# A hybrid S5 and attention layer on one core: written order kept on TensorE alone during the projection, and casts near the attention's end fixed behind their loads

## The chip, the core and the metric

The kernel runs on one core of a Trainium2 chip. The core has five engines with a queue of their own each: TensorE (PE, matrix multiplications, with its weight loads shown as PEld), VectorE (DVE), ScalarE (ACT), GpSimd (POOL) and SyncE (SP), which here only issues transfers between the chip's memory and the core. An engine works through its queue in order: an instruction that waits for another engine or for a transfer holds everything behind it. The metric is the time of one execution in microseconds of device time.

## The reference

One step of a layer with two branches. A normalised and modulated input of 2048 + 64 rows is projected to 3080 columns: the S5 input u, two gates, q, k, v and 8 forget logits. The S5 branch (32 groups with a diagonal complex state) goes through a scan, a GELU and a gated linear unit (GLU); the attention branch has 8 heads with normalised q and k and a cumulative forget bias. Both are gated, joined, projected again and added to the input.

```python
h = _rmsnorm(x, norm_g) * (1.0 + scale[:, None, :]) + shift[:, None, :]
proj = h @ w_in
u, z_s, q, k, v, z_a, f_logit = jnp.split(proj, IN_SPLITS, axis=-1)
...
y_ssm = jax.nn.gelu(y_ssm)
y_ssm = y_ssm * jax.nn.sigmoid(y_ssm @ w_glu.astype(f32) + b_glu.astype(f32))
y_ssm = (y_ssm * jax.nn.silu(z_s.astype(f32))).astype(x.dtype)
q = _rmsnorm(q.reshape(n_b, n_t, N_HEADS, HEAD_DIM), q_norm_g)
k = _rmsnorm(k.reshape(n_b, n_t, N_HEADS, HEAD_DIM), k_norm_g)
...
cum = jnp.cumsum(logf, axis=1)
...
mixed = jnp.concatenate([y_ssm, y_att], axis=-1)
y = x + gate[:, None, :] * (mixed @ w_out)
```

## The kernel before, in words

The program text is traced in order, and then a scheduler puts each engine's instructions into a queue, by a list in which an instruction is taken when the scheduler's model holds it ready. Three means fix an order against it. `ordered()` (L331) chains the instructions of its block on every engine to one another, so that each queue is the written order. `Chain.strict` (L137) does this for TensorE alone. `keep_in_program_order` fixes a single instruction behind the one that was written before it on its engine.

The stages in the order of time:

- Up to about 130 us: loading and normalising the input, and the first u columns.
- About 130 to 808 us: `InProj.line` (L627) works through 22 stretches of the projection, each a set of 256 columns of u, k, v, q or z for half of the rows. A set of weights is loaded by `fetch` (L516) into two buffers `wst`, and cut into a high and a low part by `part` (L529), four pairs of tiles: ACT casts `whi` (L310), DVE subtracts to `wlo` (L312). A block of 128 rows takes 24 matmuls, three for each of 8 slices, and its result goes to one of three banks `low2` to `low4`. `natural` (L585) evicts k and q blocks: ACT squares (L618), DVE and POOL make the power `qss` (L317, L318), DVE multiplies (L622, L623), SP writes. It evicts v blocks by a copy (L612). `channels` (L558) evicts u (L570) and z (L580, then a write to `z_d`, L581).
- Between the blocks, `line` takes steps of `rest()`, the side work: the S5 setup and 16 sets, the end of the scan, the forget logits (with the round trip of `lf` through memory), the attention's bias, and eight steps `operands` (L1615). Each of these loads four quarter blocks `b` of the output weights (L1623), adds and subtracts them, casts them to `ph` and `pl`, and writes eight tiles `t` back to memory (L1636).
- The whole of that stands in `with e.ordered()` in the kernel before.
- From 808 us: the GLU (weights `wgs`, cast to `wgh` and `wgl`) and the attention, with TensorE strict. Here `weights` (L1644) takes steps between the attention's units: it loads blocks `ost` in a ring of three buffers, casts them on ACT to `ohb` (L310), subtracts on POOL to `olb` (L196), then does the same with `m0`, split into `mha11` and `mha21`, and with the decode rows (`decode_load`, L1815). The attention's exponentials `p` run on ACT (L343).
- From about 1311 us: the output projection, in written order on all engines.

Of the kernel before, what the change touches and what calls it, by code (L numbers as in the profile page):

```python
# [21 lines left out]
DEC = 64  # L22
# [158 lines left out]
def Step(tc, a, o, ctx):  # L181
# [3 lines left out]
    V, S, PL, PE = nc.vector, nc.scalar, nc.gpsimd, Chain(tc, nc.tensor, nosync)  # L185
# [116 lines left out]
    V.memset(lf, 0.0)  # L302
    cm = cst.tile([P, H, 21], F32, name="cm")

    def split(x, hi, lo, eh=None, el=None):
        eh = eh or S
        if eh is V:
            V.tensor_copy(hi, x)
        else:
            S.copy(hi, x)  # L310
        if el is V:
            V.tensor_tensor(lo, x, hi, op=ALU.subtract)  # L312
        else:
            padd(lo, x, hi, ALU.subtract)
# [817 lines left out]
class Attn:  # L1132
# [332 lines left out]
    def run(self, out):  # L1465
# [59 lines left out]
        while not out.near:  # L1525
            next(weights)
# [67 lines left out]
class Out:  # L1594
# [12 lines left out]
    def __init__(self, e):  # L1607
        self.e = e
        self.mem = Region(e.nc)
        self.pre = Region(e.nc, R_PRE)  # L1610
        self.b, self.a, self.x, self.acc, self.tmp, self.gate = {}, {}, {}, {}, {}, {}
        self.d = []
        self.near = False

    def operands(self, k, n):  # L1615


        e = self.e
        pre = self.pre
        ns = slice(256 * n, 256 * n + 256)  # L1620
        b11, b12, b21, b22 = (pre.tile([P, 256], F32, name="b%d%d" % (i, j), bufs=1) for i in range(2) for j in range(2))
        for i, b in enumerate((b11, b12, b21, b22)):
            e.nc.sync.dma_start(b, self.block(i // 2, i % 2, k)[:, ns])  # L1623
        yield
        yield
        t2 = pre.tile([P, 256], F32, name="t2", bufs=1)
        e.V.tensor_tensor(b22, b22, b12, op=ALU.subtract)
        e.padd(b12, b12, b11, ALU.subtract)
        e.V.tensor_tensor(t2, b22, b11, op=ALU.add)
        e.padd(b21, b21, t2, ALU.subtract)  # L1630
        yield
        for t, x in (("t3", b22), ("t1", b12), ("t2", t2), ("t4", b21)):
            hl = [pre.tile([P, 256], F32R, name="p" + i, bufs=4) for i in "hl"]
            e.split(x, *hl, el=e.V)
            for i in range(2):
                e.nc.sync.dma_start(e.t_d[t][k, i][:, ns], hl[i].bitcast(F32))  # L1636
# [7 lines left out]
    def weights(self):  # L1644


        e = self.e
        mem = self.mem
        blocks = [(i, j) for i in range(2) for j in range(2)]

        def wait(n):
            while mem.room(2048) < n:
                yield

        yield from wait(5)
        mem.ring("ost", 2048, 3)
        late = []

        def part():
            st, key = late.pop(0)  # L1660
            h, l = (mem.tile([P, 512], F32R, name="o%s%s%d" % ((x,) + key)) for x in "hl")
            e.split(st, h, l)
            self.b[key] = h, l

        for k in range(4):
            for i, j in blocks:
                yield from wait(2)
                if len(late) == 2:
                    part()
                st = mem.tile([P, 512], F32, name="ost")  # L1670
                e.nc.sync.dma_start(st, self.block(i, j, k))
                late.append((st, ("b%d%d" % (i + 1, j + 1), k)))
                yield
        while late:
            yield from wait(2)
            part()
            yield
        for x in "hl":
            for name, n in (("a11", 1), ("a12", 1), ("a22", 2), ("s4", 1)):
                yield from wait(n)  # L1680
                mem.ring("m" + x + name, 2048, n)
            mem.rings["m%sa21" % x] = mem.rings["m%ss4" % x]
        while mem.room(4096) < 2:
            yield
        for j in range(2):
            mem.ring("m%d" % j, 4096, 1)
        self.load(0, 0)
        yield
        for name in ("a11", "a21"):
            self.split(0, name)  # L1690
            yield
        for j in range(2):
            yield from wait(2)
            mem.ring("ms%d" % (j + 1), 2048, 1)
            mem.ring("m%ss1" % "hl"[j], 2048, 1)
            self.decode_load(j)
            yield
        for s in (1, 0):
            for n in (1, 0):
                if s == n == 0:  # L1700
                    yield from wait(1)
                g = self.gate[s, n] = mem.tile([P, 512], F32, tag="ost" if s or n else "gate", name="gate", bufs=1)
                e.nc.sync.dma_start(g, e.gt_d[s, 512 * n:512 * n + 512].partition_broadcast(P))
        for i in (16, 0, 1):
            while mem.room(4096) < 1:
                yield
            mem.ring("x", 4096, 1)
            self.residual(i)
            yield
        self.load(1, 0)  # L1710
        self.near = True
        for t, n in (("t2", 4), ("t1", 4), ("t3", 3)):
            for k in range(n):
                yield from wait(2)
                self.fetch(t, k)
                yield
# [42 lines left out]
        if n == 4:  # L1759
            e.V.tensor_tensor(s, a12, self.a[p, "s2"], op=ALU.subtract)  # L1760

    def split(self, p, *names):
        for name in names:
            hi, lo = (self.mem.tile([P, 4, P], F32R, tag="m" + x + name, name="m" + x) for x in "hl")
            self.e.split(self.a[p, name], hi, lo, el=self.e.V)
            self.a[p, name] = hi, lo

    def multiply(self, acc, a, b, first=True):
# [46 lines left out]
    def decode_load(self, j):  # L1815

        e = self.e
        m = self.mem.tile([P, 4, DEC], F32, tag="ms%d" % (j + 1), name="md%d" % j)
        for k in range(4):
            e.nc.sync.dma_start(m[:, k].rearrange("p (t c) -> p t c", t=TC), (e.ms_d, e.ma_d)[j][P * k:P * k + P, :, NCH:])  # L1820
        hl = self.mem.tile([P, 4, P], F32R, tag="m%ss1" % "hl"[j], name="mhl")
        e.S.copy(hl[:, :, :DEC], m)
        e.V.tensor_tensor(hl[:, :, DEC:], m, hl[:, :, :DEC], op=ALU.subtract)
        self.d.append(hl)

# [89 lines left out]
def body(tc, a, o):  # L1915
    with ExitStack() as top:
        e = Step(tc, a, o, top)
# [3 lines left out]
        ip = InProj(e)  # L1921
# [40 lines left out]
                yield from out.operands(*divmod(i, 2))  # L1962

        side = rest()
        with e.ordered():
            ts = [("u", 0, 0, (2, 3), 3, None), ("u", 256, 256, (2, 3), 3, None)]
            for half in ((2, 3), (0, 1)):
                for i, (kind, base, row) in enumerate(ip.PARTS):
                    after = (lambda g: ip.get(g - 2)) if half[0] and i == 9 else None
                    ts.append((kind, base, row, half, {"v": 2, "z": 1.5}.get(kind, 1), after))  # L1970
            ip.line(ts, side)
            left = sum(1 for _ in side)
            assert left < 12, left
            print('LEFT', left)
        at = made[0]
        low.close()
        e.psum = fixed
        e.PE.strict = True
        with ExitStack() as es:
            at.twins = e.banks(es, "twin", 2, 1024)  # L1980
            with ExitStack() as es2:
# [35 lines left out]
```

## Time and profile before

| | us |
|---|---|
| median of three runs (lowest, highest) | 1513.54 (1513.40, 1518.99) |
| the profiled execution | 1513.53 |
| its span | 1511.8 |
| around the span | 1.7 |

A row of a timeline or a chain gives the start and the length in microseconds, the engine, the line, the operation with its result and its operands, and in brackets how long the engine had been idle and what ended that. A row of the waits gives the total, how often, and the longest. "PEq" and "SPq" are the sequencers of these engines. A granted clock of 1.00 is TensorE's full speed.

### The profile page before, as it was taken

The numbers are of one execution on the slowest core, as the hardware profiler recorded it, in microseconds if no ns is written. First come the engines' busy times: TensorE is split into PE (matmuls) and PEld (weight loads), VectorE is DVE, ScalarE is ACT, GpSimd is POOL, SyncE is SP. The second block draws the span as 40 slices with busy tenths as digits, with TensorE's granted clock in tenths as the row PEclk, the third lists the DMA queues.
The fourth block names the chain that finished last, engine by engine and source line by source line (L and its number), as shares of the span: only waits on it lengthen the run. The fifth ranks groups of instructions, "written<-read, shape, count | busy, mean of one in ns | idle before, by whom it ended". The sixth has DMA issues, their size and how long they took to land.

```text
span 1511.8 us, 25816 instructions
## 1 busy us (share of the span) xinstructions
PE 1351.2 (89%) x9160; PEld 1055.0 (70%) x9160; DVE 967.3 (64%) x2404; ACT 600.3 (40%) x1641; POOL 474.5 (31%) x444
## 2 busy tenths in 40 slices
PE   5887978989999889998975989999999989798998
PEld 2885977989889788996854865555555444376887
DVE  2637857767766468654342788787687676355775
ACT  3645223444433344443322435545544435431221
POOL 1101045235312143332113312433413426324443
PEclk9899989999999899999977989999999999898999
DMA  9756312332345623433569862324122222367452
GB/s 342 298 181 183 94 43 85 122 94 86 92 122 163 232 83 96 124 105 110 174 217 287 252 169 66 92 59 134 47 64 57 57 65 72 94 205 245 158 164 87
DMA packets 249472, 204.90 MB, mean 136 GB/s; under 512 B 91295, under 2 KB 217339, under 8 KB 248320
## 3 DMA queue, kind: packets, MB, share of 16 engines
q1 hardware_dynamic: 249344, 203.27, 43.4%
q8 instruction: 72, 1.18, 0.3%
q14 instruction: 56, 0.46, 0.1%
HBM read 137.68 MB, written 65.53 MB: 134 GB/s over the span
## 4 chain that ended last, share of the span: by engine, by line
PE 46%; DMA 6%; DVE 5%; issue 2%; ACT 2%; POOL 1%; SPq 1%; ACTq 0%; DVEq 0%; POOLq 0%
PE twin L145 12%; PE bank L145 11%; PE low L145 9%; PE last L145 8%; PE glu L145 2%; DVE pb L1359 2%; PE bank L148 2%; DMA ost<-in_w_out_dram 1%; DMA wst<-in_w_in_dram 1%; DMA ms_d<-gx 1%; DMA b<-in_w_out_dram 1%; POOL olb L196 1%; DMA m<-ma_d 1%; ACT p L343 1%; DVE acc L1436 0%
## 5 line engine op out<-in xcount | busy, mean ns | idle before, releaser
L145 PE MATMUL low<-whi,h 128*128 128x256 f32 (+1 forms) x1584 | 303.7, 290 | 13.7 <-DVE ev L622 8.2
L145 PE MATMUL low<-h,whi 128*128 128x256 f32 (+2 forms) x1152 | 279.6, 335 | 17.8 <-ACT whi L310 6.2
L145 PEld LDWEIGHTS low<-whi,h 128*128 128x128 f32 x1584 | 254.6, 194 | 17.0 <-issue 9.6
L145 PE MATMUL low<-wlo,h 128*128 128x256 f32 (+1 forms) x816 | 233.1, 288 | 9.0 <-DVE wlo L312 9.0
L1359 DVE CUSTOM_DVE_ANT_0 pb<-twin,cb 128x512 bf16<-128x512 f32 (+3 forms) x328 | 200.0, 610 | 63.3 <-PE twin L145 53.9
L145 PEld LDWEIGHTS low<-h,whi 128*128 128x128 f32 x1152 | 199.4, 195 | 38.1 <-ACT whi L310 6.9
L343 ACT ACTIVATE p<-twin 128x1024 f32<-128x1024 f32 (+3 forms) x180 | 149.6, 839 | 117.6 <-PE twin L145 106.9
L145 PE MATMUL low<-h,wlo 128*128 128x256 f32 (+2 forms) x576 | 190.1, 331 | 1.0 <-DVE wlo L312 1.0
L145 PEld LDWEIGHTS low<-wlo,h 128*128 128x128 f32 x816 | 158.3, 194 | 11.2 <-DVE wlo L312 10.8
L145 PE MATMUL bank<-p,vt 128*64 128x512 f32 (+3 forms) x704 | 146.0, 538 | 0.0
L318 POOL TENSOR_TENSOR qss<-qss,mhalf 128x4 f32<-128x4 f32 (+1 forms) x68 | 76.5, 1125 | 208.7 <-DVE qss L317 207.3
L145 PE MATMUL twin<-qs,ks 64*128 64x512 f32 (+3 forms) x1056 | 134.6, 360 | 0.0
L145 PEld LDWEIGHTS low<-h,wlo 128*128 128x128 f32 x576 | 112.3, 195 | 11.0 <-DVE wlo L312 2.2
L1436 DVE TENSOR_TENSOR acc<-acc,p 128x1024 f32<-128x1024 f32 (+4 forms) x90 | 89.5, 995 | 37.5 <-ACT p L343 35.6
L312 DVE TENSOR_TENSOR wlo<-wst,whi 128x512 fp32r<-128x512 f32 (+1 forms) x96 | 70.9, 766 | 50.9 <-ACT whi L310 50.7
L145 PEld LDWEIGHTS twin<-qs,ks 64*128 64x128 f32 x1056 | 95.4, 192 | 11.2
L145 PE MATMUL twin<-sm,kb 64*128 64x512 f32 (+3 forms) x360 | 78.5, 431 | 26.5 <-DVE pm L1359 13.8
L618 ACT ACTIVATE ev<-low 128x64 f32<-128x64 f32 x256 | 53.7, 224 | 117.8 <-PE low L145 51.2
L145 PEld LDWEIGHTS bank<-p,vt 128*64 128x64 f32 x704 | 45.4, 141 | 65.5 <-issue 57.9
L145 PEld LDWEIGHTS twin<-sm,kb 64*128 64x128 f32 x360 | 34.8, 189 | 68.2 <-DVE pm L1359 33.8
L145 PE MATMUL twin<-ks,qs 64*128 64x512 f32 (+3 forms) x328 | 71.6, 436 | 6.7 <-ACT p L343 5.7
L196 POOL TENSOR_TENSOR x<-x,ot 128x512 f32<-128x512 f32 (+1 forms) x34 | 52.2, 1539 | 79.6 <-DVE ot L1734 75.6
(435 smaller groups left out, 2576.5 us busy)
## 6 DMA issues: line engine op xcount, KB each, us to landing
wst<-in_w_in_dram SPq DMA_DIRECT2D x48, 512.0 KB
x<-in_x_prompt_dram SPq DMA_DIRECT2D x32, 512.0 KB
h<-h SPq DMA_DIRECT2D x16, 1024.0 KB
wada<-in_w_ada_dram SPq DMA_DIRECT2D x12, 1024.0 KB
cb<-cb_d SPq DMA_DIRECT2D x20, 512.0 KB
out_dram<-ev SPq DMA_DIRECT2D x64, 128.0 KB
out_dram<-x SPq DMA_DIRECT2D x32, 256.0 KB
z_d<-th SPq DMA_DIRECT2D x24, 256.0 KB
```

Of the source, the lines that this page charges most:

```text
L145: return self.keep(self.pe.matmul(*a, **kw))
L148: return self.keep(self.pe.transpose(*a, **kw))
L196: PL.tensor_tensor(out, x, y, op=op)
L312: V.tensor_tensor(lo, x, hi, op=ALU.subtract)
L318: PL.tensor_tensor(out, out, bc(mhalf[:out.shape[0]], list(out.shape)), op=ALU.pow)
L343: i = S.activation(out, x, func, **kw)
L618: S.activation(tv[:, h], pv[:, h], AF.Square, accum_out=ss[:r, h:h + 1])
L1359: V.tensor_tensor_reduce(b[:, :n], ps[:, h, :n], cb[:, h, :n], 1.0, NEG, ALU.add, ALU.max, accum_out=self.pm[:, t, h, pi:pi + 1])
L1436: (PL if j else V).tensor_tensor(y[:rows, :, c0:nq], x[:rows, :, c0:nq], p[:rows, :, :n], op=ALU.add)
```

## The change

The block of the projection loses `ordered()`; TensorE alone keeps its written order there, since `strict` is set before it and not after it. The other engines' instructions come as the scheduler puts them. What is computed, and with which instructions, stays the same. Fixed one by one are the loads of the `b` quarters (L1623), and on ACT the casts of `ohb`, `mha11`, `mha21` and of the decode rows. The decode loads now come first, ahead of the splits of `m0`, and the decode casts behind them.

```diff
-    def split(x, hi, lo, eh=None, el=None):
+    def split(x, hi, lo, eh=None, el=None, keep=False):
...
-            S.copy(hi, x)
+            i = S.copy(hi, x)
+            if keep:
+                tc.keep_in_program_order(i)
...
-            e.nc.sync.dma_start(b, self.block(i // 2, i % 2, k)[:, ns])
+            e.tc.keep_in_program_order(e.nc.sync.dma_start(b, self.block(i // 2, i % 2, k)[:, ns]))
...
-            e.split(st, h, l)
+            e.split(st, h, l, keep=True)
...
         self.load(0, 0)
-        yield
-        for name in ("a11", "a21"):
-            self.split(0, name)
-            yield
         for j in range(2):
...
             self.decode_load(j)
+            yield
+        yield
+        for name in ("a11", "a21"):
+            self.split(0, name, keep=True)
+            yield
+        for j in range(2):
+            self.decode_split(j)
             yield
...
+        self.raw.append(m)
+
+    def decode_split(self, j):
+        e = self.e
+        m = self.raw[j]
         hl = self.mem.tile([P, 4, P], F32R, tag="m%ss1" % "hl"[j], name="mhl")
-        e.S.copy(hl[:, :, :DEC], m)
+        e.tc.keep_in_program_order(e.S.copy(hl[:, :, :DEC], m))
...
-        with e.ordered():
-            ts = [("u", 0, 0, (2, 3), 3, None), ("u", 256, 256, (2, 3), 3, None)]
...
-            ip.line(ts, side)
-            left = sum(1 for _ in side)
-            assert left < 12, left
-            print('LEFT', left)
+        e.PE.strict = True
+        ts = [("u", 0, 0, (2, 3), 3, None), ("u", 256, 256, (2, 3), 3, None)]
...
+        ip.line(ts, side)
+        for _ in side:
+            pass
         at = made[0]
         low.close()
         e.psum = fixed
-        e.PE.strict = True
```

Line numbers in the changed file are larger by 2 up to the class `Out` (L618 is L620 there). What the change does to the queues is shown at three places.

**The first k stretch, on POOL and DVE.** First POOL's queue before, where `qss` is the power for an eviction, and the products `b` and `tb` belong to the S5 setup.

```order
L318 TENSOR_TENSOR qss_1_2047<-qss_1_2047,mhalf_0_112 128x4
L196 TENSOR_TENSOR tb_0_2223<-bb_0_1204,qim_0_2143 128x512
L196 TENSOR_TENSOR b_124288_0_2221<-ba_0_1203,qre_0_2142 128x512
L196 TENSOR_TENSOR b_124288_0_2221<-b_124288_0_2221,tb_0_2223 128x512
L196 TENSOR_TENSOR tb_0_2223<-ba_0_1203,qim_0_2143 128x512
L196 TENSOR_TENSOR b_126336_0_2222<-bb_0_1204,qre_0_2142 128x512
L196 TENSOR_TENSOR b_126336_0_2222<-b_126336_0_2222,tb_0_2223 128x512
L318 TENSOR_TENSOR qss_2_2088<-qss_2_2088,mhalf_0_112 128x4
```

The same queue now; the last row is the first `qss` of the program.

```order
L196 TENSOR_TENSOR b_126336_0_2222<-b_126336_0_2222,tb_0_2223 128x512
L964 MEMSET bp_0_2471 128x64
L965 COPY bp_0_2471<-b_124288_0_2221 128x2x16
L944 TENSOR_TENSOR si_0_2352<-ta_119936_0_1409,tb_117888_0_1408 128x2x256
L942 TENSOR_TENSOR tmp_0_2354<-ta_122112_0_1410,tb_115840_0_1407 128x512
...
L957 TENSOR_TENSOR si_0_2352<-si_0_2352,tmp_0_2354 128x2x256
...
L320 TENSOR_TENSOR qss_0_2008<-qss_0_2008,mhalf_0_112 128x4
```

The six products stood among the powers; now they, and the first wide operations of the S5 sets, stand ahead of all powers. DVE's queue at the last weights ahead of the first k block, before (`ta`, `cm` and `cn` belong to the tables of the S5 setup):

```order
L766 TENSOR_TENSOR ta_122112_0_1410<-ta_122112_0_1410,cn_166464_0_1366 128x32x2
L312 TENSOR_TENSOR wlo_2_220<-wst_0_207,whi_2_219 128x528
L312 TENSOR_TENSOR wlo_3_224<-wst_1_209,whi_3_223 128x528
L312 TENSOR_TENSOR wlo_4_564<-wst_1_209,whi_4_563 128x528
L766 TENSOR_TENSOR cm_166976_0_1373<-ta_122112_0_1410,wim_0_1412 128x128
```

And now, with `co`, `lin` and `btt` of the first S5 set:

```order
L946 TENSOR_TENSOR co_0_2351<-ta_119936_0_1409,tb_115840_0_1407 128x2x256
L953 TENSOR_TENSOR lin_0_2432<-pim_0_1324,b_126336_0_2222 128x2x128
L954 TENSOR_TENSOR btt_0_2431<-pre_0_1323,b_124288_0_2221 128x256
L946 TENSOR_TENSOR co_1_2701<-ta_119936_0_1409,tb_115840_0_1407 128x2x256
L768 TENSOR_TENSOR un_176320_0_1773<-un_176320_0_1773,uo_176448_0_1774 128x32
L314 TENSOR_TENSOR wlo_2_220<-wst_0_207,whi_2_219 128x528
L955 TENSOR_TENSOR btt_0_2431<-btt_0_2431,lin_0_2432 128x256
L314 TENSOR_TENSOR wlo_3_224<-wst_1_209,whi_3_223 128x528
```

The end of the S5 setup has moved ahead of these subtractions.

**A change of weights, on ACT.** Before, from the last casts of one set of weights to the first cast of the next one (`ev` are evictions, `both` is the short block of the 64 decode rows):

```order
L310 CAST whi_2_219<-wst_1_209 128x2x256
L606 COPY both_0_2335<-low_136 64x256
L618 ACTIVATE ev_1_2021,qss_1_2047<-both_0_2335 64x64 x4
L946 COPY co_1_2701<-ta_119936_0_1409 128x2
L946 COPY si_1_2702<-ta_122112_0_1410 128x2
L612 COPY ev_2_2060<-low_140 128x256
L612 COPY ev_3_2101<-low_132 128x256
L310 CAST whi_3_223<-wst_0_207 128x2x256
```

And now:

```order
L310 CAST whi_2_219<-wst_1_209 128x2x256
L608 COPY both_0_2335<-low_136 64x256
L1082 COPY rot_0_2347<-si_0_2352 128x2
L620 ACTIVATE ev_1_2021,qss_1_2047<-both_0_2335 64x64 x4
L310 CAST whi_3_223<-wst_0_207 128x2x256
L614 COPY ev_2_2060<-low_140 128x256
L614 COPY ev_3_2101<-low_132 128x256
```

The cast `whi_3` has moved ahead of two evictions. It is so, by one or two, at nearly every change of weights.

**The attention's end, on ACT.** Before, from two exponentials `p` on (`sm` is a copy of sums):

```order
L343 ACTIVATE p_1_8912<-twin_8883 128x1024
L310 CAST ohb_170240_0_12541<-ost_0_12348 128x512
L1314 COPY sm_1_8031<-bank_77 73x512
L343 ACTIVATE p_2_8931<-twin_8016 128x1024
L343 ACTIVATE p_3_8951<-twin_8020 128x1024
L310 CAST ohb_91648_0_12604<-ost_0_12348 128x512
L343 ACTIVATE p_4_8978<-twin_8883 128x1024
L343 ACTIVATE p_5_9016<-twin_8016 128x2x384
L310 CAST ohb_34304_0_12642<-ost_0_12348 128x512
```

And now:

```order
L1316 COPY sm_1_8031<-bank_77 73x512
L345 ACTIVATE p_2_8931<-twin_8016 128x1024
L345 ACTIVATE p_3_8951<-twin_8020 128x1024
L310 CAST ohb_197760_0_12376<-ost_0_12348 128x512
L310 CAST ohb_9728_0_12382<-ost_1_12350 128x512
L345 ACTIVATE p_4_8978<-twin_8883 128x1024
L345 ACTIVATE p_5_9016<-twin_8016 128x2x384
L310 CAST ohb_13824_0_12420<-ost_2_12380 128x512
```

Before, the last three of sixteen casts are seen here; now the first three are, two casts between two pairs of exponentials.

More of the change, by code (lines that the diff above doesn't have):

```diff
@@ L1611, in __init__ @@
         self.b, self.a, self.x, self.acc, self.tmp, self.gate = {}, {}, {}, {}, {}, {}
-        self.d = []
+        self.d, self.raw = [], []
         self.near = False
@@ L1760, in differ, with split @@
             e.V.tensor_tensor(s, a12, self.a[p, "s2"], op=ALU.subtract)
-    def split(self, p, *names):
+    def split(self, p, *names, keep=False):
         for name in names:
             hi, lo = (self.mem.tile([P, 4, P], F32R, tag="m" + x + name, name="m" + x) for x in "hl")
-            self.e.split(self.a[p, name], hi, lo, el=self.e.V)
+            self.e.split(self.a[p, name], hi, lo, el=self.e.V, keep=keep)
             self.a[p, name] = hi, lo
@@ L1964, in body @@
         side = rest()
-        with e.ordered():
-            ts = [("u", 0, 0, (2, 3), 3, None), ("u", 256, 256, (2, 3), 3, None)]
[L1967 to L1970, printed above, removed]
-            ip.line(ts, side)
-            left = sum(1 for _ in side)
-            assert left < 12, left
-            print('LEFT', left)
+        e.PE.strict = True
+        ts = [("u", 0, 0, (2, 3), 3, None), ("u", 256, 256, (2, 3), 3, None)]
+        for half in ((2, 3), (0, 1)):
+            for i, (kind, base, row) in enumerate(ip.PARTS):
+                after = (lambda g: ip.get(g - 2)) if half[0] and i == 9 else None
+                ts.append((kind, base, row, half, {"v": 2, "z": 1.5}.get(kind, 1), after))
+        ip.line(ts, side)
+        for _ in side:
+            pass
         at = made[0]
```

## Prediction

> **What bounds the kernel now.** I read the page first. TensorE (PE) is busy for 89% of the span and no other engine comes near it.
>
> ```profile
> span 1511.8 us, 25816 instructions
> PE 1351.2 (89%) x9160; PEld 1055.0 (70%) x9160; DVE 967.3 (64%) x2404; ACT 600.3 (40%) x1641; POOL 474.5 (31%) x444
> ```
>
> The change leaves TensorE's work as it is, so all it can win is TensorE's idle time and the clock that goes with it. The second view is therefore the table of windows, which shows where that idle time lies (columns: window, its length, busy time of PE, its weight loads, DVE, ACT and POOL, then the granted clock, DMA share and GB/s).
>
> ```profile
> 130.00:723.00 593.00, 545.42 (x3826) 506.29 (x3819) 391.11 (x1141) 238.10 (x1046) 190.03 (x236) 0.96 0.37 110
> 180.00:205.00 25.00, 25.00 (x204) 25.00 (x203) 15.29 (x60) 8.52 (x55) 5.16 (x5) 1.00 0.28 81
> 205.00:230.00 25.00, 17.25 (x110) 16.48 (x109) 14.63 (x32) 6.95 (x47) 16.34 (x15) 0.73 0.22 67
> 723.00:816.00 93.00, 66.81 (x269) 51.93 (x267) 35.47 (x72) 24.49 (x56) 17.45 (x23) 0.85 0.68 217
> 1190.00:1310.00 120.00, 98.23 (x719) 51.03 (x717) 74.27 (x164) 52.28 (x77) 50.63 (x32) 0.90 0.31 81
> ```
>
> The stretch that loses its written order is 130 to 723 us (the projection with the S5 work beside it) and 723 to 816 us (the last eight steps of side work). In the first PE is idle for 593 − 545.4 = 47.6 us, and the clock of 0.96 costs another 0.04 × 593 = 23.7 us. The two rows of 25 us show how idle time and clock go together: without a gap 204 matmuls and clock 1.00, with gaps 110 matmuls and clock 0.73. The third view says what PE waited for in 130 to 723 us (total, times, longest).
>
> ```profile
> PE low L145 <- DVE wlo L312: 10.0, 9, 2.8
> PE low L145 <- DVE ev L622: 8.2, 2, 5.5
> PE low L145 <- DMA lf<-out_dram: 4.8, 1, 4.8
> PE bank L148 <- DVE btt L953: 4.5, 1, 4.5
> PE low L145 <- POOL bp L963: 3.2, 2, 2.3
> PE low L145 <- DVE th L580: 2.9, 1, 2.9
> PE bank L145 <- ACT bt L973: 2.7, 4, 1.7
> PE low L145 <- ACT whi L310: 2.5, 3, 1.2
> PE low L145 <- ACT bt L973: 2.5, 5, 0.8
> PE low L145 <- DVE ca L953: 1.8, 2, 1.0
> PE low L148 <- DVE cx L1196: 1.8, 1, 1.8
> ```
>
> These eleven rows hold 44.9 of the 47.6 us. They fall into two kinds. Work that was ready but queued behind something unrelated: ev, btt, bp, th, both bt, ca and cx, 8.2 + 4.5 + 3.2 + 2.9 + 2.7 + 2.5 + 1.8 + 1.8 = **27.6 us**. Work that hangs on a load: wlo, whi and lf, 10.0 + 2.5 + 4.8 = **17.3 us**. The longest wait of the first kind can be followed in POOL's and DVE's timelines (start, length, idle time before it in brackets):
>
> ```profile
> 206.09 1.06 POOL L196 TENSOR_TENSOR tb<-bb,qim 128x512 f32<-128x512 f32 x1
> 211.94 1.26 POOL L196 TENSOR_TENSOR b<-b,tb 128x512 f32<-128x512 f32 x1
> 214.21 0.42 DVE L622 TENSOR_TENSOR ev<-low,qss 128x256 f32<-128x256 f32 x1 [4.48 <-POOL qss L318]
> ```
>
> Six wide multiplications of the S5 setup stand on POOL ahead of a tiny power `qss` that an eviction needs; DVE waits 4.48 us for it, and PE for DVE.
>
> **The projection without written order.** For that place the order is certain: POOL now does the six multiplications ahead of the first `qss`, DVE does the chain that feeds them earlier, and the 5.5 us wait goes. For the rest of the first kind, a queue in the order of readiness takes away a wait if the readiness is foreseen well. Nothing in the trace shows how well; the bounds are none of it and all of it, 0 and 27.6 us. I take three quarters, **20.7 us**, because the one wait that I can follow row by row goes wholly, and the others have the same form. Of the load kind I take one third, **5.8 us** (bounds 0 and 17.3): loads are now issued about one block earlier, but the wait for `lf` is a round trip through memory that stays.
>
> What the change adds is in the ACT queue: the first cast of the next weights now stands one or two evictions earlier, close behind its load. ACT did wait for these loads before:
>
> ```profile
> L310 ACT CAST whi<-wst 128x512 fp32r<-128x512 f32 (+1 forms) x76 | 45.1, 625 | 29.6 <-DMA wst<-in_w_in_dram 23.8 <-PE low L145 5.4
> 750.87 6.82 DMA wst<-in_w_in_dram
> ```
>
> 23.8 us of such waiting on ACT cost PE only the 2.5 us of the whi row and part of the 10.0 of the wlo row, because finished blocks lay ahead. Behind an earlier cast stand evictions, and an eviction's chain through ACT, DVE and POOL takes 192.27 − 189.39 = 2.9 us:
>
> ```profile
> 189.39 0.16 DVE L610 TENSOR_TENSOR lf<-low,bfb 128x8 f32<-128x8 f32 x1
> 190.55 0.17 DVE L317 TENSOR_SCALAR qss<-qss 128x4 f32<-128x4 f32 x1 [1.00 <-ACT ev L618]
> 191.85 0.42 DVE L622 TENSOR_TENSOR ev<-low,qss 128x256 f32<-128x256 f32 x1 [0.77 <-POOL qss L318]
> ```
>
> A block of 24 matmuls takes 24 × 25.0 / 204 = 2.94 us, and with three banks PE can run two more blocks before it needs the first one's bank: 5.9 − 2.9 = 3.0 us of slack. A load of 6.82 us with a cast of 0.62 us holds the queue 7.44 us when the cast stands straight behind the issue (4.4 us past the slack), 1.5 us past it with one block between, and nothing with two. The bounds for the 22 sets of weights are 0 and 22 × 4.4 = 97 us; the trace is nearest to the lower end (7 waits and almost no loss), so I take a little over a third of a microsecond each, **8 us**. In it is also one place at about 185 us: on DVE the last wide multiplications of the S5 setup now stand ahead of three `wlo` subtractions that PE needs there.
>
> That leaves 20.7 + 5.8 − 8 = 18.5 us of idle time, 39% of 47.6. The clock should follow in proportion, 0.39 × 23.7 = 9.2 us. Together **28 us** (bounds: a loss of 39 us, rival 4 below, and a gain of 50 with all of the first kind, a third of the second and the clock in proportion, 27.6 + 5.8 + 16.6).
>
> The Trainium skill, TensorE: Matmul & The Clock Gate, Part 1, says that the clock halves only after an idle window of about 3.4 us. By it only the waits of 5.5, 4.8 and 4.5 us would cost clock, two of the three go, and the clock would give 15.8 us in place of 9.2, a sum 7 us lower; the trace speaks partly for it (0.73 around the 5.5 us wait). The skill also has a rule against the change: SBUF — State Buffer, Who interferes with whom, says that a DVE instruction with two SBUF inputs and a GpSimd instruction that reads SBUF block each other wholly. Two rows agree, one operation held while POOL ran wide additions, and its group of four (shortest, median, longest in ns):
>
> ```profile
> 256.05 3.84 DVE L622 TENSOR_TENSOR ev<-both,qss 64x256 f32<-64x256 f32 x1 [0.90 <-POOL qss L318]
> L622 DVE TENSOR_TENSOR ev<-both,qss x4: 418/1291/3843, 223.2 to 390.5; 64x256 f32<-64x256 f32 x4
> ```
>
> By that rule freed queues collide more often, and three such holds on the path, each 3.84 − 0.42 = 3.4 us, would take back 10 us; the sum would be 10 us higher.
>
> **The last eight steps, 723 to 816 us.** Each loads four tiles `b`, combines and casts them, and writes eight transposed tiles `t`. SP's timeline and the chain of waits show the first step, a usual one, and the end:
>
> ```profile
> 723.19 1.92 SPq L1623 DMA_DIRECT2D b<-in_w_out_dram  x4
> 738.84 1.84 SPq L1623 DMA_DIRECT2D b<-in_w_out_dram  x4
> 747.99 1.37 SPq L1623 DMA_DIRECT2D b<-in_w_out_dram  x3
> 799.86 7.29 DMA cb<-cb_d
> 809.63 4.75 DMA wgs<-in_w_glu_dram
> ```
>
> A usual step takes 747.99 − 738.84 = 9.2 us and the first 15.7, because its casts stood behind an eviction of a gate block; they now stand ahead of it, 6 us. SP spreads the gate's writes better, 2 us. Against that the load `wgs`, for which PE waits here, now stands behind several transfers `cb`, each like the one of 7.29 us: 5 us. Sum **3 us** (bounds −5 and 8: all of the loss alone, all of the gain alone). Faster blocks of the gate do not help, since SP's chain sets this end.
>
> **The attention's end, 1190 to 1310 us.** PE's waits there, and two casts that cause them:
>
> ```profile
> PE twin L145 <- ACT p L343: 18.1, 7, 6.2
> 1287.81 0.62 ACT L310 CAST ohb<-ost 128x512 fp32r<-128x512 f32 x1 [5.74 <-DMA ost<-in_w_out_dram]
> 1301.93 1.14 ACT L310 CAST mha<-m 128x512 fp32r<-128x512 f32 x2 [7.48 <-DMA m<-ms_d]
> 1272.85 2.38 POOL L1436 TENSOR_TENSOR acc<-p,p 128x1024 f32<-128x1024 f32 x1
> 1288.51 1.27 POOL L196 TENSOR_TENSOR olb<-ost,ohb 128x512 fp32r<-128x512 f32 x1 [3.70 <-ACT ohb L310]
> ```
>
> A cast that waits for its load blocks the exponentials `p` behind it, 18.1 us in seven waits. Pinned, the casts come in pairs between pairs of exponentials, and the `mha` casts after the last one. The loads are then early for the first three only: each later one needs a buffer that a cast and a POOL subtraction (1.27 us) have released, while POOL also has sums of 2.38 us to do. I keep a third of the waits, 6 us, and take **12 us** of gain (bounds 0 and 18.1). The cover here is POOL's queue; if it falls behind, the casts wait again and the exponentials with them.
>
> In the first 130 us a few transposes change places on TensorE and three small loads move ahead; the nearest rows give nothing that is waited for, so 0 (−5 to 5).
>
> **Sum.** 28 + 3 + 12 = 43 us, of the profiled execution's 1511.8 + 1.7 = 1513.5 us, which is also the median of the three runs (1513.54): **1470 us**.
>
> **Rivals.**
> (1) Queues fit almost perfectly: 50 in the projection, 8 in the last steps, 18 at the attention's end, 1437 us. For it speaks that all eight queue waits are of work that was ready; against it that `lf` and the `ost` ring remain.
> (2) The projection's waits only change places (0 of 28, 0 of 3) and the attention's end gains its 12: 1501 us. For it speaks that DVE is busy for 391 of 593 us, so that something is always ahead of something.
> (3) Casts of the next weights stand straight behind their loads in 12 of the 22 stretches: 12 × 4.4 = 53 us. Without the 8 us above, the gains are 26.5 + 0.56 × 23.7 + 15 = 55 us, so 1511 us, no change.
> (4) The other side, the same place with another answer to where the load is issued: where its buffer comes free late, in 18 of the 22 stretches, 18 × 4.4 = 79 us are lost against 55, **1538 us** (39.7 − 79 = −39 for the projection alone). It is slower than before by over 0.5% once more than (55 + 7.6) / 4.4 = 14 stretches are hit. Against it: ACT's seven waits of 23.8 us so far, with a loss of 2.5.
>
> **How the numbers follow.** Forecast 0.50 (own range 1450 to 1490), rival 1 0.10, rival 2 0.12, rival 3 0.11, rival 4 0.17. Half a per cent, 7.6 us, is about what a measurement of this kernel can tell from no change. Faster: 0.50 + 0.10 + 0.12 = 0.72; same 0.11; slower 0.17. The range reaches from rival 1 to just past rival 3, 1437 to 1515 us, and leaves out rival 4 and a little below.
>
> **What would show it.** Right: no wait of PE for `ev` near 214 us, the clock in 205 to 230 us near 1.00, PE's idle time in the projection down from 47.6 to about 29 us, the waits for `p` down from 18.1 to about 6. Wrong: ACT's time in front of `whi` for the load `wst` well above 23.8 us with PE waiting for `ev` at each change of weights (rivals 3 and 4), PE waiting for `wlo` by several microseconds near 185 us, or a start of the gate's matmuls that is not earlier than the projection's gain.

## Result, and the profile after

The changed kernel takes 1472.32 us (median of 4 runs, 1467.23 to 1473.36), the kernel before 1515.72 us (1513.40 to 1518.99) in the same comparison. The ratio is 0.9705, with a 95% interval of 0.9673 to 0.9738. The profiled execution has a span of 1471.1 us against 1511.8, 40.7 us less; the medians differ by 43.4 us, and the forecast was 43 us. One of the executions reported below is left out of its median and ratio: with ACT in written order (experiment 2) one of four took 3190.09 us, the others 1488.36 to 1489.04, and no trace of it was kept.

The table of windows, cut at the events that end each stage (first load of a quarter `b`, first matmul of the GLU, end), for the kernel after. The columns are window, length, then busy time and instructions of PE, PEld, DVE, ACT and POOL, granted clock, DMA share, GB/s.

```profile
130.00:695.57 565.57, 534.60 (x3810) 497.86 (x3811) 392.38 (x1138) 243.56 (x1042) 202.15 (x236) 0.97 0.39 115
695.57:792.26 96.69, 60.87 (x267) 49.04 (x265) 35.65 (x66) 23.79 (x54) 17.41 (x22) 0.84 0.78 243
792.26:1471.10 678.84, 638.33 (x4440) 420.82 (x4440) 486.80 (x1061) 272.23 (x410) 260.69 (x150) 0.97 0.40 118
```

And the same stages of the kernel before:

```profile
130.00:723.19 593.19, 545.61 (x3826) 506.45 (x3819) 391.30 (x1144) 238.29 (x1046) 190.03 (x236) 0.96 0.37 110
723.19:815.55 92.36, 66.17 (x266) 51.32 (x264) 35.28 (x70) 24.04 (x55) 17.08 (x22) 0.85 0.68 216
815.55:1511.80 696.25, 644.99 (x4440) 423.13 (x4440) 481.31 (x1061) 271.89 (x410) 254.13 (x150) 0.95 0.41 120
```

A window's length less PE's busy time is PE's idle time. PE does the same 9160 matmuls in both executions; the first window holds 16 fewer, nearly all because 14 more run in the 130 us ahead of it (647 in place of 633).

| stage | forecast | measured | of it idle | of it busy |
|---|---|---|---|---|
| projection, 130 us to the first load `b` | −28 | −27.6 | −16.6 | −11.0 |
| last eight steps, to the first GLU matmul | −3 | +4.3 | +9.6 | −5.3 |
| GLU, attention and output | −12 | −17.4 | −10.8 | −6.7 |
| sum | −43 | −40.7 | −17.8 | −23.0 |

The total is near the forecast because two errors, of 7.3 and of 5.4 us, nearly cancel. Most of the shorter busy time is the clock. In windows of one microsecond, PE's busy time times what the granted clock lacks to 1.00 adds up to 20.6 us in the projection before and 11.6 now, to 4.5 and 0.0 in the last steps, and to 26.0 and 19.1 behind them: 8.9, 4.5 and 6.9 us less, 20.3 of the 23.0. The rest is mainly the 16 matmuls. (The mean of 0.84 for the last steps now does not speak against it: it holds a long wait in which the clock is 0.50, while the matmuls there ran at 1.00.) So about half of what was won is clock, not idle time.

PE's waits in the projection after the change (total, times, longest), to be read against the eleven rows of before:

```profile
PE low L145 <- DVE th L582: 10.1, 2, 9.3
PE low L145 <- DVE wlo L314: 6.9, 9, 1.9
PE low L145 <- DMA lf<-out_dram: 5.6, 1, 5.6
PE low L145 <- DVE ev L624: 4.2, 2, 3.6
PE bank L145 <- ACT bt L975: 1.9, 6, 0.5
PE low L145 <- ACT bt L975: 1.4, 5, 0.4
```

The rows btt, bp, ca and cx have gone. Work queued behind other work falls from 27.6 to 10.1 + 4.2 + 1.9 + 1.4 = 17.6 us, and work that hangs on a load from 17.3 to 12.5 us. One new row leads the list, `th`, almost all of it one wait of 9.3 us at 490 to 499 us. The profile's chain into that wait begins with a load of weights and the cast behind it on ACT, and goes on through evictions, the S5 work of a set on DVE and a write of `ev` (the second row is from ACT's timeline):

```profile
478.92 8.73 DMA wst<-in_w_in_dram
487.67 0.62 ACT L310 CAST whi<-wst 128x512 fp32r<-128x512 f32 x1 [2.42 <-DMA wst<-in_w_in_dram]
```

What became of the rest is in PE's waits of the whole execution after:

```profile
PE glu L145 <- ACT wgh L310: 35.8, 1, 35.8
PE twin L145 <- ACT p L345: 6.3, 5, 2.0
PE last L145 <- DVE mhs L1833: 4.5, 1, 4.5
PE bank L145 <- DVE acc L1438: 3.0, 1, 3.0
```

PE is through with its gate blocks earlier and then waits 35.8 us at the GLU, where it waited 14.1 us before: SP's chain of eight steps sets that point. The waits for the exponentials `p` are 6.3 us, as forecast (18.1 before, 6 expected).

### The profile page after: what moved, and what is told of

Read it like the earlier page. It is cut to its first block, busy times and chain, and to the rows that moved or that the text cites. A ratio compares the mean times of both kernels' runs of the same rounds, so it can differ in the third digit from the quotient of the medians.

```text
span 1471.1 us, 25856 instructions
## 1 busy us (share of the span) xinstructions
PE 1329.3 (90%) x9160; PEld 1040.8 (71%) x9160; DVE 976.3 (66%) x2404; ACT 607.5 (41%) x1640; POOL 493.0 (34%) x444
## 4 chain that ended last, share of the span: by engine, by line
PE 67%; DVE 10%; DMA 9%; SPq 4%; issue 4%; ACT 3%; POOL 2%; DVEq 0%; ACTq 0%; POOLq 0%
PE low L145 30%; PE bank L145 12%; PE twin L145 12%; PE last L145 9%; DMA x<-in_x_prompt_dram 3%; PE glu L145 3%; DVE pb L1361 2%; PE bank L148 2%; SPq L402 1%; DMA b<-in_w_out_dram 1%; DVE acc L1438 1%; DMA wst<-in_w_in_dram 1%; DMA ost<-in_w_out_dram 1%; SPq L1625 1%; POOL olb L196 1%
## 5 line engine op out<-in xcount | busy, mean ns | idle before, releaser
L145 PE MATMUL low<-whi,h 128*128 128x256 f32 (+1 forms) x1584 | 297.1, 286 | 14.4 <-DVE th L582 10.1
L145 PE MATMUL low<-h,whi 128*128 128x256 f32 (+2 forms) x1152 | 275.4, 331 | 6.2 <-ACT th L572 5.8
L145 PEld LDWEIGHTS low<-whi,h 128*128 128x128 f32 x1584 | 249.4, 191 | 17.0 <-DVE th L582 10.8
L145 PE MATMUL bank<-p,vt 128*64 128x512 f32 (+3 forms) x704 | 141.5, 524 | 0.0
L310 ACT CAST whi<-wst 128x512 fp32r<-128x512 f32 (+1 forms) x96 | 58.0, 625 | 64.4 <-DMA wst<-in_w_in_dram 48.9
L620 ACT ACTIVATE ev<-low 128x64 f32<-128x64 f32 x256 | 53.6, 224 | 67.7 <-PE low L145 29.2
```

What stands on the lines that cost most here:

```text
L145: return self.keep(self.pe.matmul(*a, **kw))
L310: i = S.copy(hi, x)
L620: S.activation(tv[:, h], pv[:, h], AF.Square, accum_out=ss[:r, h:h + 1])
```

## The experiments

Each was timed against the kernel before on the same chip; the medians of that lie at 1512 to 1516 us, so small differences between kernels of different groups are not to be read. A queue is called free here when its order is the scheduler's.

**1. The two parts apart.** First the changed kernel with the attention's end put back:

```diff
-            e.split(st, h, l, keep=True)
+            e.split(st, h, l)
...
         self.load(0, 0)
+        yield
+        for name in ("a11", "a21"):
+            self.split(0, name)
+            yield
...
-            yield
-        yield
-        for name in ("a11", "a21"):
-            self.split(0, name, keep=True)
-            yield
-        for j in range(2):
...
-        e.tc.keep_in_program_order(e.S.copy(hl[:, :, :DEC], m))
+        e.S.copy(hl[:, :, :DEC], m)
```

> The projection freed as in the change, the attention's end as before it. Theory (the two parts are independent, and the sum is made of a projection that ends 27.6 us earlier, eight last steps that give back 4.3 us, and an attention's end with its own 17 us): 1513.5 - 27.6 + 4.3 = 1490 us, PE's waits for the exponentials p near 18 us as before. Rival (the casts had to be fixed because a free projection moves them to worse places): well above 1495 us, waits for p above 25 us. Second rival (the attention's end got faster because the projection ends earlier): about 1473 us, waits for p near 6 us.

Measured: 1489.11 us (1487.93 to 1491.74), ratio 0.9842 (0.9813 to 0.9871). The first `b` load is at 695.60 us, the GLU at 792.26 us, and the waits for `p` are back:

```profile
PE twin L145 <- ACT p L345: 19.3, 8, 6.4
```

Then the reverse, the projection in written order with the new attention's end:

```diff
-        e.PE.strict = True
-        ts = [("u", 0, 0, (2, 3), 3, None), ("u", 256, 256, (2, 3), 3, None)]
+        with e.ordered():
+            ts = [("u", 0, 0, (2, 3), 3, None), ("u", 256, 256, (2, 3), 3, None)]
...
+        e.PE.strict = True
```

The loads of `b` are not fixed one by one here, since the block orders them.

> Only the attention's end as in the change, the projection in written order. Theory (independent parts): 1513.5 - 17.4 = 1496 us, and the projection's waits of 47.6 us as before; the part from the first matmul of the GLU to the end takes 679 us in place of 696. Rival (only the waits for p go, the clock and the output projection do not follow): 1513.5 - 12 = 1501.5 us. Second rival (the gain comes with the projection's): 1513 us.

Measured: 1496.17 us (1494.36 to 1500.00), ratio 0.9889 (0.9858 to 0.9921). The GLU starts at 815.06 us and what follows takes 1496.0 − 815.06 = 680.9 us, with 5.3 us of waits for `p`. Both expectations held. The parts are independent as far as the medians tell: 1515.1 − 1489.1 = 26.0 and 1515.1 − 1496.2 = 18.9 us make 44.9 us together, and the whole change brings 43.4 us by its medians. Neither the claim that the free projection spoils the casts nor the claim that the attention's end gains only through the projection stands.

**2. Whose freedom matters.** Four kernels with one engine in written order in the projection (`ordered` limited to that engine, the rest as changed; shown for POOL):

```diff
-        ip.line(ts, side)
-        for _ in side:
-            pass
+        with e.ordered(mybir.EngineType.Pool):
+            ip.line(ts, side)
+            for _ in side:
+                pass
```

POOL:

> The changed kernel with POOL alone back in written order in the projection. Theory (POOL's written order, the setup's products ahead of a power that an eviction needs, cost the longest wait of 5.5 us, the rows bp 3.2 us, and their part of the clock): the projection 10 to 15 us longer; since the GLU then still starts after the same chain of last steps, the time is 1482 to 1488 us. Rival (POOL's order does not matter once the others are free): 1470 to 1475 us, no wait for ev near 214 us.

DVE:

> The changed kernel with DVE alone back in written order in the projection. Theory (the gain of the projection comes from the queues on which the waiting work stood: DVE's waits btt 4.5, ca 1.8 and cx 1.8 and the ev wait that DVE passes on; with DVE in written order the S5 setup also ends as late as before): the projection about 12 us longer, the time 1480 to 1486 us. Rival (as with POOL, whose written order made the kernel 9 us faster: a written order on one engine costs nothing so long as ACT and SP are free): 1463 to 1473 us.

ACT:

> The changed kernel with ACT alone back in written order in the projection. Theory (ACT's waits bt 5.2 us of before, and evictions behind S5 work): 1476 to 1482 us. Rival (the earlier casts of the next weights in the free order cost more than they bring; ACT waited 40.7 us for the loads wst in place of 23.8): 1465 us or below. Second rival (ACT's order makes no difference, PE's waits for bt and whi change by under 3 us): 1470 to 1474 us.

SP:

> The changed kernel with the order of transfers (SP) alone as written in the projection and the last steps. Theory (writes that wait for a result hold the loads of the weights and of the S5 sets behind them; this is what kept the others waiting): 1485 us or above, with PE waiting for th, wlo and lf as before. Rival (SP's order matters only in the last steps, where the free order put wgs behind cb and vt): 1465 to 1472 us, with the GLU starting earlier after the first load b than 96.7 us.

| in written order | time, us | ratio (interval) | first load `b` | GLU starts |
|---|---|---|---|---|
| none (the change) | 1472.32 | 0.9705 (0.9673 to 0.9738) | 695.57 | 792.26 |
| POOL | 1463.55 | 0.9674 (0.9646 to 0.9702) | 688.83 | 786.05 |
| SP | 1474.74 | 0.9727 (0.9706 to 0.9749) | 698.93 | 795.38 |
| ACT | 1488.74 | 0.9820 (0.9787 to 0.9854) | 707.05 | 807.14 |
| DVE | 1489.46 | 0.9827 (0.9803 to 0.9851) | 723.34 | 810.92 |
| all (the attention's end alone) | 1496.17 | 0.9889 (0.9858 to 0.9921) | 723.04 | 815.06 |

The expectation for POOL failed, and in sign: its first `b` load comes 6.7 us earlier than with POOL free, and its time is 8.8 us lower (1463.15 to 1465.99 against 1467.23 to 1473.36), though the intervals of the two ratios overlap. Of the 9.6 us between the two profiled spans, 3.4 lie behind the start of the GLU, where nothing was changed. So no gain from POOL's freedom shows; that written order is better for it rests on one profile of each. The expectations for DVE (1480 to 1486) and ACT (1476 to 1482) named the side but came out too low, and for SP neither fits: its projection is 3.4 us longer, and the stretch from `b` to the GLU is the same 96.5 us as in the change. With DVE alone in written order the projection's whole gain is gone (723.34 against 723.19 before). PE's two longest rows of waits there, in 130 to 723 us:

```profile
PE low L145 <- DVE wlo L314: 17.0, 10, 6.0
PE low L145 <- DVE ev L626: 11.8, 11, 3.3
```

The wait of 6.0 us ends at 221 us, when the first of three `wlo` is there. They stand on DVE behind an eviction that itself waits, 1.00 us for ACT's `ev` and 0.69 us for POOL's `qss`:

```profile
218.03 0.42 DVE L626 TENSOR_TENSOR ev<-low,qss 128x256 f32<-128x256 f32 x1 [0.69 <-POOL qss L320]
219.47 4.68 DVE L314 TENSOR_TENSOR wlo<-wst,whi 128x512 fp32r<-128x512 f32 x3
```

Over the projection DVE waits 52.3 us in 35 waits for ACT's `ev` ahead of `qss` in this kernel, and 16.8 us in 25 in the changed one:

```profile
DVE qss L319 <- ACT ev L622: 52.3, 35, 5.8
DVE qss L319 <- ACT ev L620: 16.8, 25, 1.2
```

So DVE in written order stands still in front of one eviction's step while weights for the next blocks are queued behind it. That this is all of the 27.8 us is not shown.

What POOL's freedom costs shows in two windows of that kernel and of the changed one (the changed one second):

```profile
130.00:200.00 70.00, 69.91 (x536) 65.61 (x529) 51.87 (x298) 22.33 (x86) 7.97 (x14) 0.96 0.37 94
200.00:300.00 100.00, 91.80 (x708) 87.06 (x707) 83.27 (x194) 46.86 (x215) 50.85 (x58) 0.97 0.31 93
```

```profile
130.00:200.00 70.00, 65.75 (x475) 60.00 (x476) 61.27 (x293) 22.04 (x77) 23.02 (x26) 0.93 0.37 89
200.00:300.00 100.00, 93.33 (x723) 89.19 (x722) 73.52 (x186) 45.16 (x215) 42.18 (x49) 0.98 0.30 89
```

In 130 to 200 us 536 matmuls run in place of 475, and DVE takes 51.9 us for 298 operations in place of 61.3 us for 293. Free POOL does 23.0 us of work there, POOL in written order 8.0. The price is paid later, in 200 to 300 us, at the place of the prediction; PE's timeline with POOL in written order:

```profile
214.06 0.55 PE L145 MATMUL low<-whi,h 128*128 128x256 f32 x1 [6.41 <-ACT ev L622]
```

The wait of 5.5 us near 214 us, which the prediction was sure of, is back as 6.4 us, as the queue says it must be. It costs less than what the early POOL work costs, which is paid at two places of the changed kernel. The first is the six products of the S5 setup, which POOL now runs from 147 to 156 us. Beside them six small operations of the setup on DVE take 0.94 to 1.34 us each in place of about 0.2, some 5.5 us more in all, and the first `wlo` behind them starts at 160.79 us in place of 155.35 with POOL in written order. PE waits for it, and the clock falls (the last two rows are 160 to 170 us, first for the changed kernel, then with POOL in written order):

```profile
149.25 0.94 DVE L768 TENSOR_TENSOR un<-un,uo 128x32 f32<-128x32 f32 x1
154.79 1.29 POOL L196 TENSOR_TENSOR b<-b,tb 128x512 f32<-128x512 f32 x1
154.80 1.34 DVE L768 TENSOR_TENSOR un<-wa 128x32 f32<-128x32 f32 x1
161.53 0.39 PE L145 MATMUL low<-h,wlo 128*128 128x256 f32 x1 [1.86 <-DVE wlo L314]
160.00:170.00 10.00, 8.09 (x53) 7.89 (x54) 8.37 (x45) 1.28 (x3) 0.00 (x0) 0.83 0.64 179
160.00:170.00 10.00, 10.00 (x87) 10.00 (x86) 7.38 (x42) 2.02 (x5) 0.00 (x0) 1.00 0.54 163
```

That is 34 of the 61 matmuls that 130 to 200 us lack. The second place is near 185 us; DVE and POOL there in the changed kernel:

```profile
182.76 1.09 DVE L768 TENSOR_TENSOR un<-wre 128x32 f32<-128x32 f32 x1
...
186.67 1.31 DVE L768 TENSOR_TENSOR un<-un,uo 128x32 f32<-128x32 f32 x1
187.91 0.69 DVE L314 TENSOR_TENSOR wlo<-wst,whi 128x528 fp32r<-128x528 f32 x1
```

```profile
182.65 1.15 POOL L944 TENSOR_TENSOR si<-ta,tb 128x512 f32<-128x512 f32 x1 [10.02 <-DVE ta L768]
...
184.94 2.99 POOL L957 TENSOR_TENSOR si<-si,tmp 128x512 f32<-128x512 f32 x1
```

An operation on 128x32 elements that takes 0.19 us otherwise takes 1.09 us here beside a POOL operation of 1.15 us, and POOL's second step for `si` takes 2.99 us. Behind them stand the three `wlo` that PE needs.

**3. Which part of DVE's order.** DVE in written order only after the S5 setup, and only in it:

```diff
+        for x in e.nc.cur_bb.bb.instructions[marks[0]:]:
+            if x.engine == mybir.EngineType.DVE:
+                if last:
+                    tc.add_manual_dep(x, last, e.PE.dep)
+                last = x.name
```

For the setup alone the instructions are those from the start of the projection up to this mark. They hold what the projection's own blocks put on DVE in that time, too.

> The changed kernel with DVE in written order from the end of the S5 setup on; the setup's own order is free. DVE in written order throughout gave 1489.5 us and took the whole gain of the projection. Theory (DVE's gain is in the steady part, where S5 work of a set stands between an eviction's steps and ahead of wlo): 1483 to 1489 us. Rival (the gain is that the setup's chain ends before the first k block): 1473 to 1477 us.

> The changed kernel with DVE in written order in the S5 setup only, free after it. Theory (the steady part carries the gain; in the setup the free order also costs, with DVE operations held while POOL runs near 185 us): 1468 to 1476 us. Rival (the setup carries it): 1483 us or above.

Measured: 1485.17 us (1480.38 to 1489.78) with the first `b` load at 717.11 us, and 1482.31 us (1482.14 to 1482.47) with it at 707.65 us. The first is as the theory had it; the second lies between theory and rival, so neither was right alone. In the profiles, written order costs 717.11 − 695.57 = 21.5 us after the setup and 707.65 − 695.57 = 12.1 us in it. Both parts carry. Which one carries more is open: the first kernel's four times fall into two pairs (1480.38 and 1481.08, 1489.26 and 1489.78), the profile is of the slowest, and the intervals of the ratios overlap (0.9768 to 0.9859 and 0.9761 to 0.9829). The sum, 33.6 us, is above the 27.8 us of the whole, so they are not quite independent, or the 21.5 us is too large.

**4. The chain of the last steps.** One number changed: more side work per gate block in the first half, so that the eight steps begin earlier.

```diff
-                ts.append((kind, base, row, half, {"v": 2, "z": 1.5}.get(kind, 1), after))
+                ts.append((kind, base, row, half, {"v": 2, "z": 2 if half[0] else 1.5}.get(kind, 1), after))
```

> The changed kernel with more side work per block in the gate's stretches of the first half (two steps per unit of size in place of one and a half), so that the eight last steps begin some blocks earlier. Theory (after the change SP's chain of these steps, and the load wgs behind it, set the start of the GLU, and PE waits 35.8 us for them): most of the 35.8 us goes, 1440 to 1450 us. Rival (the load wgs waits for something else, the writes of the gate or the loads cb and vt): PE still waits over 25 us, 1465 to 1473 us. Second rival (more side work per block stalls the first half's gate blocks by as much): wait at the GLU gone, but 1465 us or more, with PE's new waits in 400 to 490 us.

Measured: **1434.82 us** (1431.15 to 1438.43), ratio 0.9481 (0.9443 to 0.9519), faster than the theory's 1440 to 1450. Its first `b` load is at 638.14 us, the GLU starts at 755.50 us, and in between PE is no longer idle; its waits for the GLU there are 1.4 us:

```profile
638.14:755.50 117.36, 113.00 (x563) 94.10 (x562) 52.82 (x106) 38.85 (x131) 30.94 (x32) 0.99 0.70 222
```

```profile
PE glu L145 <- DVE th L582: 1.4, 1, 1.4
```

The eight steps still take their time, 117 us from the first load to the GLU, but 563 matmuls lie beside them where there were 267. The second rival's stall in the first half did not come: PE is busy for 96.46 of 100 us in 400 to 500 us, where the changed kernel has 88.71.

With POOL in written order as well:

> More side work per block in the gate's stretches of the first half (1434.8 us by itself) and POOL in written order in the projection (9 us faster than the changed kernel by itself). Theory (the two gains are of different places, and the start of the GLU no longer hides the projection's): 1424 to 1430 us. Rival (POOL's written order helped through the last steps, which no longer set the end): 1433 to 1437 us.

Measured: 1435.43 us (1432.96 to 1436.81), ratio 0.9466 (0.9443 to 0.9489): no further gain. But the rival's reason is wrong too: POOL's order had helped in the projection (`b` at 688.83), and here the first `b` load is at 638.02 us against 638.14. In 130 to 200 us it is still ahead (545 matmuls against 483), and it loses that again up to 638 us. Why it keeps the lead in the one kernel and not in the other is open.

**5. The attention's end in two.** Only the sixteen casts `ohb` fixed (the edit is against the first kernel of experiment 1), and only the decode loads first with the splits behind:

```diff
-            e.split(st, h, l)
+            e.split(st, h, l, keep=True)
```

> Projection as in the change; at the attention's end only the sixteen casts ohb fixed behind their loads, the splits of m0 and the decode rows as before the change. Between 1489.1 us (nothing fixed) and 1472.3 us (all). Theory (what stalls the exponentials are casts that wait for ost; the m0 casts give one wait of 6 us): 1476 to 1480 us, waits for p 10 to 13 us with one of 6 us left. Rival (the order of loads matters, decode first): 1484 to 1489 us.

The reverse leaves this line as it was and keeps the rest of the change:

> Projection as in the change; at the attention's end the decode loads first and the splits of m0 and of the decode rows fixed, the sixteen casts ohb free. Theory: the wait of 6 us for the m0 casts goes, the waits for ost stay, 1480 to 1484 us, waits for p near 12 us. Rival: 1473 to 1477 us, most of the gain.

Measured: 1474.64 us (1473.19 to 1476.41), ratio 0.9741 (0.9700 to 0.9782), and 1476.57 us (1474.28 to 1478.86), ratio 0.9757 (0.9721 to 0.9793). Both theories were too pessimistic, and for the second the rival's time is what came; each edit alone brings most of the 1489.11 − 1472.32 = 16.8 us. They do it in different ways, as PE's waits from 800 us on show, with the casts fixed first and with the decode part second:

```profile
PE last L145 <- DVE ot L1803: 5.6, 1, 5.6
PE bank L145 <- DVE z L1453: 3.2, 1, 3.2
PE last L145 <- DVE mhs L1831: 3.0, 1, 3.0
...
PE twin L145 <- ACT p L345: 2.3, 3, 1.6
```

```profile
PE twin L145 <- ACT p L345: 11.2, 7, 4.3
PE last L145 <- DVE mhs L1833: 4.5, 1, 4.5
```

With the casts alone, the waits for `p` nearly vanish, and what is left are 3.2 us for `z` in the attention and 5.6 + 3.0 us in the output stage. With the decode part alone, 11.2 us of waits for `p` stay and the output stage's wait for `ot` is gone.

## Why the prediction came out right, step by step

- **What bounds the kernel.** Right: TensorE's idle time and its clock hold the whole result. Over the whole span idle time fell by 18.8 us (160.6 to 141.8) and busy time by 21.9 (1351.2 to 1329.3).
- **Projection, queue waits and new waits, 20.7 − 8 = 12.7 us.** 27.6 fell to 17.6 us, 10.0 us less. Apart from the new wait of 9.3 us for `th` it fell to 8.3, so both sizes are near what was forecast; the reasons are not. The argument for "three quarters" was the one wait that could be followed by rows, and that was the wrong one to reason from. The wait near 214 us did go, and clock and matmuls in 205 to 230 us rose from 0.73 and 110 to the row below, but POOL's new order does not carry the gain: with POOL as written the kernel is not slower. DVE's order carries it: all 27.8 us are lost with DVE as written, and 11.5 us with ACT as written. That the size came near is luck.

```profile
205.00:230.00 25.00, 22.90 (x189) 22.11 (x188) 16.51 (x42) 9.84 (x70) 12.08 (x11) 1.00 0.27 83
```

- **Projection, load waits, 5.8 us.** Measured 4.8.
- **The mechanism of the new waits.** It was to be the casts close behind their loads. ACT did wait longer for the weights:

```profile
ACT whi L310 <- DMA wst<-in_w_in_dram: 40.7, 15, 6.2
```

  That is 40.7 us in 15 waits, where it was 23.8 in 7. The number of stretches lies between the 12 of rival 3 and the 18 of rival 4, but a wait is 2.7 us on average, below the 3.0 us of slack that the prediction worked out, in place of a held queue of 7.44 us. PE's row for `whi` is gone, its row for `wlo` fell from 10.0 to 6.9 us, and ACT in written order is slower by 11.5 us up to the first `b` load. What can be seen of a price is the chain into the wait of 9.3 us, where a cast's wait of 2.42 us is one link; how much of the 9.3 us is due to it is open. So neither rival came. The place at 185 us was real, 185 matmuls in 180 to 205 us in place of 204; the larger one of this kind, at 161 us, was not foreseen.
- **The clock, 9.2 us.** Measured 8.9 in the projection. The base of 23.7 us counted the low clock of idle time as a cost too; 20.6 us of busy time were lost to it. The Trainium skill's rule (TensorE: Matmul & The Clock Gate, Part 1), as the prediction applied it, would have had 15.8. The trace does not agree: there were three waits of more than 3.4 us before (5.5, 4.8 and 4.5) and there are three now (9.3, 5.6 and 3.6), and near 161 us two waits of 1.86 and 0.37 us are followed by a clock of 0.50 from 164 to 166 us.
- **The skill's rule against the change** (SBUF — State Buffer, Who interferes with whom). It was weighed at 10 us and left out of the sum. The trace agrees with it at 149 to 156 and at 182 to 190 us, though an operation with one input, `un<-un` at 150.23 us, was held as well (0.97 us for 0.18). It is the likeliest reason why POOL's freedom does not help; no run here isolates its price from the rest of POOL's order.
- **Last eight steps, −3 us.** Wrong in sign, +4.3. The first step did shrink, from 15.7 to 705.34 − 695.57 = 9.8 us. What failed is the term for the transfers ahead of `wgs`, taken as 5 us, and the 2 us for better spread writes, which do not show. SP's chain at the end:

```profile
767.56 1.82 SPq L1625 DMA_DIRECT2D b<-in_w_out_dram  x4
...
770.47 1.69 SPq L1266 DMA_DIRECT2D cb<-cb_d  x3
...
772.72 1.00 SPq L1303 DMA_DIRECT2D vt<-in_cache_v_dram  x1
773.77 2.77 SPq L1303 DMA_DIRECT2D vt<-out_dram  x2
776.64 2.94 SPq L1638 DMA_DIRECT2D t<-ph  x1
...
785.49 0.53 SPq L1550 DMA_DIRECT2D wgs<-in_w_glu_dram  x1
```

  The attention's loads also stand ahead of the last step's writes `t`, not just of `wgs`: the last step takes 782.87 − 767.56 = 15.3 us to its last write. Before, the last step took 808.10 − 796.97 = 11.1 us. The six steps between take 62.2 us in place of 58.1, and from the last write to the GLU it is 9.4 us in place of 7.5. That makes 4.2 + 4.1 + 1.9 = 10.2 us lost against 5.9 won by the first step. The statement beside it, that faster gate blocks do not help because SP's chain sets this end, was right, and was worth more than the forecast made of it: 35.8 us of PE's time lay there, and experiment 4, which took all but 1.4 of it away, brought 37.5 us.
- **Attention's end, −12 us.** The waits were right, 18.1 to 6.3 us. The size of the gain was not: the sum had no clock for this stage, although its window stood at 0.90. Busy time fell by 6.7 us from the GLU to the end. The output stage's wait for `ot` of 6.7 us went, and two new ones came, 3.0 us for the attention's last sums and 4.5 us in the output stage. The idle time that went, 10.8 us, is near the 12 forecast; the rest of the 17.4 is the clock that was left out.
- **What was to be seen.** All four signs came: no wait of PE near 214 us, a clock of 1.00 in 205 to 230 us, 31.0 us of idle time in the projection (about 29 forecast) and 6.3 us of waits for `p`. They were signs of the sum, though, and not of its causes: the first two speak of POOL's queue, which experiment 2 shows not to carry the gain.
- **First 130 us.** Near 0: they hold 94.4 us of PE's work before and 95.5 after, with 14 matmuls more.

## What to carry to other kernels

A written order on every engine is one decision for each engine: try them one by one, since here DVE's cost all of the stage's gain, and POOL's brought nothing when it was freed. When a stage gets faster, look at what its end then waits for before forecasting the sum: 35.8 us, nearly as much as the change brought, lay behind a chain of transfers that did not get shorter, and one number that started the chain earlier won them. When idle time falls in a stage whose granted clock is below one, the clock belongs into the sum.

## What was not expected of the hardware

Small VectorE operations of the setup took 0.94 to 1.34 us in place of about 0.2 us while POOL ran wide operations, and POOL's took up to 3.06 us in place of 1.24 (`b`) and 2.99 in place of a mean of 1.35 (`si`). One group of DVE shows it over the projection, first before, then after (line, operation, count, busy time and mean in ns):

```profile
L956 DVE TENSOR_TENSOR co<-co,tmp 128x512 f32<-128x512 f32 x16 | 12.4, 772 | 0.0
```

```profile
L958 DVE TENSOR_TENSOR co<-co,tmp 128x512 f32<-128x512 f32 x16 | 21.6, 1347 | 0.3
```

The same sixteen operations take 21.6 us in place of 12.4 us, 18.5 with POOL in written order and 10.9 with DVE in written order. What runs beside them is the likeliest reason. The second surprise is how much of an idle microsecond comes back as clock: over the whole span 18.8 us less idle time went with 21.9 us less busy time for the same 9160 matmuls.
